# Stepwise mixers, other projection groups and PSUM scratch in a two-layer hybrid trunk

## The chip, the cores and the metric

The kernel runs on one core of one Trainium2 chip. The metric is the time of one execution in device microseconds. Engines are named as in the profile: PE is TensorE, DVE VectorE, ACT ScalarE, POOL GpSimd, SP SyncE, whose queue issues nearly all DMAs. "Lnn" is a line of the kernel.

## The reference

256 tokens of width 2048 go through two layers. Each layer: a modulation from a condition `c` (adaLN: six vectors of 2048 from one product with `ada_w`), RMSNorm, one input projection whose columns feed three mixers side by side, head norm and gates, one output projection, and an MLP with squared ReLU. Everything is fp32.

```python
def hybrid_mixer(h, positions, w_in, conv_w, ..., merge_scale, w_out):
    proj = h @ w_in
    (rq, rk, rv, rg, fq, fk, fv, ff, mq, mk, mv, mo, mi, mf) = jnp.split(proj, IN_SPLIT_IDX, axis=-1)
    y_ret = head_norm(retention(heads(rq), heads(rk), heads(rv), positions)) * jax.nn.silu(rg)     # 4 heads
    y_fox = head_norm(forgetting_attention(heads(fq), heads(fk), heads(fv), ff + fox_f_bias))      # 8 heads
    mqk = jax.nn.silu(causal_conv(jnp.concatenate([mq, mk], axis=-1), conv_w, conv_b))
    mq, mk = jnp.split(mqk, 2, axis=-1)
    y_m = head_norm(mlstm(heads(mq), heads(mk), heads(mv), mi + ..., mf + ...)) * jax.nn.sigmoid(mo)  # 4 heads
    y = jnp.concatenate([y_ret, y_fox, y_m], axis=-1) * merge_scale
    return y @ w_out
```

## The kernel before

**Products.** Activations lie transposed, 16 feature tiles of 128 x 256 tokens. Each fp32 product is made of three passes over rounded halves: an operand is split into a high part and the remainder, and TensorE adds high x low, low x high and high x high. Weights come as 512 KB chunks of two feature tiles by 512 columns (`chunk`): SP issues the DMA into one of six `raw` buffers, ACT rounds to `wh` (L228), and DVE or POOL subtracts to `wl` (L234); `pool_*` in `CFG` is POOL's share. A block is 512 output columns: form B (`mm_b`, L259 to L261) takes 12 matmuls of 256 columns for each feature tile, form A (`mm_a`, L270 to L272, for v, g and o blocks) six of 512.

**Modulation.** One tile of 128 values of `c @ ada_w` is two DMAs of 512 KB into one of four `ada` buffers (the first four halves go to `raw`), and two DVE instructions L292 that multiply by the broadcast condition and sum up. `mod_fix` folds the partial sums on PE (L302, L303) and ends on DVE (L307) or ACT (L305). Tiles wait in a list; `pump` issues them at a rate set by `ada_*` and calls `mod_fix` as soon as a set is issued.

**Order.** `run` first sums the squares of x (L364 to L369, over partitions with ones on PE, L377), forms 1/rms by three Newton steps on DVE (`newton`, L351 to L353), and spreads it with two matmuls (L395). `layer` then goes through w_in in groups of feature tiles, so that it can begin with the first tiles before the whole modulation is there: `h_make` normalises and modulates the group's tiles (L471, L476) and splits them into `hh` and `hl` (L479); `gate_mm` multiplies them with the 76 gate columns; then each of the 14 blocks but the `late` ones takes its partial product, and DVE adds it to the block's sum in SBUF, in two halves of 512 (L521). The late blocks run over all 16 tiles after that. With the last group the mixers start: convolution (L673), gates (L538 to L557), the heads of retention, mLSTM and fox, one PSUM bank `mx` for each head at a time (scores, transposes L635, values L596), `head_norm` with statistics (L708, L709) and normalisation on ACT (L724), `head_out` with transposes on PE (L738) and a merge on DVE (L741). Then come w_out in four blocks with the residual (L750), the first MLP product in two groups, and the rest of the MLP. In layer 1 the input projection is one group and POOL takes no subtractions.

A scheduler orders the instructions of each engine when the kernel is built, from the written order and its own cost estimates; `high_priority` around `mixers` and `gates` moves these ahead, `WIN` holds an ada DMA behind a weight DMA. Each engine then works its row strictly in order.

**Buffers.** PSUM has eight banks of 512 columns: four `pj` (two for each block), two for the condition, two `mx` for everything small.

## Time and profile before

| | |
|---|---|
| time, median of 3 runs | 2559.64 us (2557.45 to 2563.83) |
| profiled execution, time / span | 2560.86 / 2559.1 us |
| PE busy | 2437.6 us (95%), 18996 matmul records |
| DVE busy | 1576.2 us (62%) |
| ACT busy | 1188.3 us (46%) |
| POOL busy | 843.5 us (33%) |
| DMA | 630.46 MB, mean 246 GB/s |
| mean granted clock of PE | 0.98 |

Busy time is a share of the whole span; what an engine costs a stage is read from windows of that stage. Ends of matmuls are modelled: at full flow their records overlap, so PE's time for one is taken from counts in a full window. PEclk is the clock that the throttle granted, 1.00 being 2.4 GHz and half of it the lower level.

### The profile page before, as it was taken

To read this page: it belongs to the slowest core of one execution; us is meant where nothing else is said; L and a number is where in the kernel's file an instruction comes from. 1 tells how busy PE (TensorE), PEld (TensorE's weight loads), DVE (VectorE), ACT (ScalarE), POOL (GpSimd) and SP (SyncE) were. 2 spreads that over 40 slices of the span, in tenths; PEclk is the share of its full clock that TensorE was granted. 3 is DMA by queue.
4 is the path that set the end of the run, shared out by engine and by line. 5 is a ranking of instruction groups with operands and counts; after the bars stand their busy time and mean duration, and the time that the engine had idled before them with its cause. 6 is when DMAs were issued, how large, how long until landed. Compare 5 with 4: busy or idle time off the path is not lost.

```text
span 2559.1 us, 46654 instructions
## 1 busy us (share of the span) xinstructions
PE 2437.6 (95%) x18996; PEld 2365.6 (92%) x18996; DVE 1576.2 (62%) x2468; ACT 1188.3 (46%) x1502; POOL 843.5 (33%) x350
## 2 busy tenths in 40 slices
PE   6999897798999999999999999999999999999997
PEld 5899775798999999999998899989999999999997
DVE  6886985888565453334368976566755554554555
ACT  5444444445553444443455554454654444344443
POOL 4777762234676667666661000000000000000000
PEclk9999997899999999999999999999999999999999
DMA  9899765898999987777776778555555555555553
GB/s 340 301 331 332 232 232 192 316 340 313 346 334 327 333 307 271 262 275 275 261 248 236 253 243 296 173 170 177 187 184 183 187 182 184 187 183 184 186 184 106
DMA packets 177824, 630.46 MB, mean 246 GB/s; under 512 B 19652, under 2 KB 25158, under 8 KB 177608
## 3 DMA queue, kind: packets, MB, share of 16 engines
q1 hardware_dynamic: 177176, 627.08, 70.7%
q8 instruction: 149, 2.44, 0.4%
q14 instruction: 67, 0.55, 0.1%
q10 hardware_dynamic: 432, 0.39, 0.1%
HBM read 625.30 MB, written 2.10 MB: 245 GB/s over the span
## 4 chain that ended last, share of the span: by engine, by line
PE 80%; DVE 11%; issue 2%; POOL 2%; DMA 2%; ACT 2%; SPq 0%; DVEq 0%; POOLq 0%; ACTq 0%
PE pj L260 23%; PE pj L259 23%; PE pj L261 22%; DVE ada L292 3%; PE pj L270 2%; PE pj L271 2%; PE pj L272 2%; POOL wl L234 2%; DMA ada<-ada_w 2%; DVE wl L234 1%; DVE cv L673 1%; PE mx L596 1%; DVE blk L521 0%; DVE blk L417 0%; ACT wh L228 0%
## 5 line engine op out<-in xcount | busy, mean ns | idle before, releaser
L228 ACT CAST wh<-raw 128x1024 fp32r<-128x1024 f32 (+1 forms) x808 | 841.1, 1042 | 1131.1 <-PE pj L261 931.3
L234 POOL TENSOR_TENSOR wl<-raw,wh 128x1024 fp32r<-128x1024 f32 x345 | 840.9, 2444 | 516.7 <-ACT wh L228 506.3
L234 DVE TENSOR_TENSOR wl<-raw,wh 128x1024 fp32r<-128x1024 f32 (+1 forms) x463 | 569.7, 1231 | 550.6 <-ACT wh L228 548.9
L260 PE MATMUL pj<-hh,wl 128*128 128x256 f32 x2912 | 823.0, 285 | 10.3 <-DVE wl L234 7.6
L261 PE MATMUL pj<-hh,wh 128*128 128x256 f32 x2912 | 820.0, 284 | 0.0
L259 PE MATMUL pj<-hl,wh 128*128 128x256 f32 x2912 | 799.5, 285 | 19.9 <-DVE blk L521 9.6
L260 PE MATMUL pj<-blk,wl 128*128 128x256 f32 x2528 | 706.8, 282 | 1.9 <-DVE wl L234 1.9
L261 PE MATMUL pj<-blk,wh 128*128 128x256 f32 x2528 | 704.3, 281 | 0.0
L259 PE MATMUL pj<-blk,wh 128*128 128x256 f32 x2528 | 691.9, 282 | 1.9 <-ACT blk L518 1.5
L260 PEld LDWEIGHTS pj<-hh,wl 128*128 128x128 f32 x2912 | 562.6, 193 | 11.9 <-DVE wl L234 8.2
L259 PEld LDWEIGHTS pj<-hl,wh 128*128 128x128 f32 x2912 | 549.7, 193 | 23.7 <-DVE hl L479 7.8
L261 PEld LDWEIGHTS pj<-hh,wh 128*128 128x128 f32 x2912 | 562.3, 193 | 0.3
L292 DVE SCALAR_TENSOR_TENSOR ada<-ada,cond 128x1024 f32<-128x1024 f32 x380 | 455.7, 1213 | 169.1 <-DMA ada<-ada_w 167.9
L260 PEld LDWEIGHTS pj<-blk,wl 128*128 128x128 f32 x2528 | 477.2, 189 | 2.5 <-DVE wl L234 2.5
L261 PEld LDWEIGHTS pj<-blk,wh 128*128 128x128 f32 x2528 | 477.9, 189 | 0.0
L259 PEld LDWEIGHTS pj<-blk,wh 128*128 128x128 f32 x2528 | 468.3, 189 | 2.5 <-ACT blk L518 1.8
L1005 POOL TENSOR_TENSOR blk<-blk,R 128x1024 f32<-128x1024 f32 x1 | 2.3, 2346 | 1192.0 <-ACT R L399 1192.0
L750 DVE SCALAR_TENSOR_TENSOR X<-pj,mod,X 128x256 f32<-128x256 f32 x284 | 118.2, 476 | 61.3 <-PE pj L261 61.1
L271 PE MATMUL pj<-wl,hh 128*128 128x512 f32 x384 | 154.3, 402 | 0.8 <-POOL wl L234 0.7
L272 PE MATMUL pj<-wh,hh 128*128 128x512 f32 x384 | 152.4, 397 | 0.0
L270 PE MATMUL pj<-wh,hl 128*128 128x512 f32 x384 | 143.8, 401 | 5.3 <-DVE blk L521 3.9
L521 DVE SCALAR_TENSOR_TENSOR blk<-pj,blk 128x512 f32<-128x512 f32 x110 | 74.0, 683 | 38.8 <-PE pj L261 29.0
(216 smaller groups left out, 1672.2 us busy)
## 6 DMA issues: line engine op xcount, KB each, us to landing
raw<-w_ff SPq DMA_DIRECT2D x508, 512.0 KB, 4.1
ada<-ada_w SPq DMA_DIRECT2D x380, 512.0 KB, 6.2
raw<-w_in SPq DMA_DIRECT2D x224, 512.0 KB, 4.9
raw<-w_out SPq DMA_DIRECT2D x64, 512.0 KB, 5.1
X<-x SPq DMA_DIRECT2D x4, 512.0 KB, 6.9
raw<-ada_w SPq DMA_DIRECT2D x4, 512.0 KB, 10.0
raw<-w_ff SPq DMA_DIRECT2D x8, 256.0 KB, 3.6
out<-blk SPq DMA_DIRECT2D x4, 512.0 KB, 3.6
```

Of the source, the lines that this page charges most:

```text
L228: nc.scalar.copy(hi, raw)
L234: eng.tensor_tensor(lo, raw, hi.bitcast(F32), ALU.subtract)
L259: nc.tensor.matmul(o, lhsT=wh[:, s], rhs=al, start=st, stop=False, skip_group_check=True)
L260: nc.tensor.matmul(o, lhsT=wl[:, s], rhs=ah, start=False, stop=False, skip_group_check=True)
L261: nc.tensor.matmul(o, lhsT=wh[:, s], rhs=ah, start=False, stop=last, skip_group_check=True)
L270: nc.tensor.matmul(o, lhsT=al[:, s], rhs=wh, start=first, stop=False)
L271: nc.tensor.matmul(o, lhsT=ah[:, s], rhs=wl, start=False, stop=False)
L272: nc.tensor.matmul(o, lhsT=ah[:, s], rhs=wh, start=False, stop=last)
L292: nc.vector.scalar_tensor_tensor(raw, raw, 1.0, self.cond, ALU.mult, ALU.mult, accum_out=self.part[l][:, i, h:h + 1])
L521: nc.vector.scalar_tensor_tensor(d, p, scale, d, ALU.mult, ALU.add)
L596: nc.tensor.matmul(ps[:, i * P:i * P + P], lhsT=lt, rhs=v[:, j, c:c + P], start=first, stop=last, skip_group_check=True)
L750: V.scalar_tensor_tensor(self.X(k), ps[n // 2][:, n % 2 * T:n % 2 * T + T], self.mod[l][:, c:c + 1], self.X(k), ALU.mult, ALU.add)
```

## The change

- The groups of w_in in layer 0 are 2, 2, 2, 4 and 6 tiles instead of 2, 2, 2, 2, 4, 4, with 12 blocks in each instead of 11: `fv1` is no longer late. Rates of modulation tiles and POOL's shares change (`CFG`).
- The first four modulation tiles (two of scale, two of shift) are computed on PE: `ada_first`, 64 matmuls of one column from weights laid out anew (`ada_0`), eight DMAs of 512 KB that use four `raw` and four `ada` buffers. The ada halves that went to `raw` are gone.
- `pump` leaves `mod_fix` to `flush`, which runs at the next step; the h tiles of the other early tiles are made there.
- A block's two banks are one tile `pj` of 1024 columns, and its sum is one DVE instruction (or one ACT copy) of 1024 columns instead of two of 512.
- `gate_mm` runs once, in the last group. Gates, Newton chains, head norm statistics and the first layer's h tiles have operands in `mx` banks in PSUM instead of SBUF.
- The mixers are generators. `tick` moves up to two of them a step after each chunk of two tiles in `proj`, and in w_out; w_out's products call `tick` until the group that they need is there. The priorities, `DEFER`, `EARLY` and `BEHIND` are gone.

```diff
-CFG = [dict(win=[2, 2, 2, 2, 4, 4], late=3, lead_win=False, ada_win=[4, 4, 4, 8, 8, 16], ada_late=0, ada_out=36,
+CFG = [dict(win=[2, 2, 2, 4, 6], late=2, lead_win=False, ada_win=[4, 4, 8, 12, 14], ada_late=4, ada_out=19,
             ff1=[8, 8], ff1_blocks=6, early_ff1=[[0, 1]], stat_ff1=(0, 1), ada_ff1=[16, 16], ada_ff=48,
-            pool_win=1.0, pool_out=0.5, pool_ff=0.8),
+            ..., ada_ff=60,
+            pool_win=[1.0, 1.0, 1.0, 1.0, 0.5], pool_late=0.5, pool_out=0.3, pool_ff1=[0.3, 0.8], pool_ff=0.8),
...
-NPJ = 4
-DEFER = ("fv1",)
+LANES = 2
-EARLY = 4
-BEHIND = 6
-PRI = dict(mix=1000)
...
     def pump(self, n):
+        self.flush()
...
             if last:
-                self.mod_fix(l, j, kts, {1: C_NMIX, 4: C_NMLP}.get(j))
+                self.fixes.append((l, j, kts))
...
+    def flush(self):
+        while self.fixes:
+            l, j, kts = self.fixes.pop(0)
+            self.mod_fix(l, j, kts, {1: C_NMIX, 4: C_NMLP}.get(j))
+            if (l, j) == (0, 0):
+                self.h_make(0, 0, 1, kts, True)
+
+    def ada_first(self, kts):
+        nc = self.nc
+        ps = self.bank((P, 512))
+        n = len(kts)
+        for i in range(2 * n):
+            for h in range(2):
+                raw = (self.raw if h else self.adap).tile([P, 8, P], F32, tag="raw" if h else "ada", name=self.name("raw"))
+                nc.sync.dma_start(raw, self.io["ada_0"][:, i, 8 * h:8 * h + 8, :])
+                for k in range(8):
+                    nc.tensor.matmul(ps[:, i:i + 1], lhsT=raw[:, k, :], rhs=self.ccol[:, 8 * h + k:8 * h + k + 1],
+                                     start=i == 0 and h == 0 and k == 0, stop=False, skip_group_check=True)
...
+        nc.vector.scalar_tensor_tensor(a[:, KT + kts[0]:KT + kts[0] + n], ps[:, 0:n], 1.0,
+                                       self.vcol(0, C_NMIX + kts[0], n), ALU.add, ALU.mult)
+        nc.scalar.copy(a[:, kts[0]:kts[0] + n], ps[:, n:2 * n])
...
-    def newton(self, v, shape):
+    def newton(self, v, shape, ps, scale=None):
...
+        y = ps[:, :n] if len(shape) == 2 else ps[:, :n].rearrange("p (a b) -> p a b", b=shape[2])
...
     def proj(...):
...
+            w = self.chunk(self.io["w_in"][l, b, k0 // 4][:, r0:r0 + 2, :], 2)
...
+            if late:
+                self.step()
+            self.tick()
...
-            for d, p in zip(self.halves(dst), ps):
-                nc.vector.scalar_tensor_tensor(d, p, scale, d, ALU.mult, ALU.add)
+            d = self.flat(dst)
+            nc.vector.scalar_tensor_tensor(d, ps, scale, d, ALU.mult, ALU.add)
...
     def fox(...):
...
+            yield True
             for b in range(3):
                 nc.tensor.transpose(ps[:, b * P:b * P + P], p[:, b * P:b * P + P], self.ident)
             V.tensor_copy(p, ps[:, 0:384])
+            yield True
             self.pv(ps, p, v, h * P)
             self.u_out(U, h, ps)
+            yield True
...
-        return U, rs
+        self.head_norm(U, rs)
+        yield False
+        yield from self.head_out(l, U, None, 1 + g)
...
     def head_norm(self, U, rs):
-        mv = self.small.tile([P, 2, 4, 2], F32, name="mv")
+        ps = self.bank((P, 512))
+        mv = ps[:, 0:16].rearrange("p (a b c) -> p a b c", b=4, c=2)
...
+    def tick(self):
+        n = 0
+        for t in list(self.tasks):
+            if n == LANES:
+                break
+            r = next(t, None)
+            if r is None:
+                self.tasks.remove(t)
+            else:
+                n += r
...
             if last:
-                with self.tc.high_priority(offset=PRI["mix"]):
-                    self.gates(l, gps)
+                self.gates(l, self.gate_mm(l))
...
                 w = self.chunk(io["w_out"][l, nb, kc], 4)
+                while kc not in self.Y:
+                    self.tick()
...
+                    if j % 2 == 1:
+                        self.tick()
```

The order of the built kernels at three places follows. Tiles are named with numbers; a name keeps its buffer kind (`raw`, `ada`, `mx`, `pj`, `blk`).

DVE before, at the start: the last two of eight ada halves, and what leads to `hl`, which the first w_in matmul reads.

```order
L292 SCALAR_TENSOR_TENSOR ada_195,part_124<-ada_195,cond 128x1024
L292 SCALAR_TENSOR_TENSOR ada_198,part_124<-ada_198,cond 128x1024
L234 TENSOR_TENSOR wl_215<-raw_212,wh_214 128x152
L471 TENSOR_TENSOR ht_206<-X_91,R 128x512
L471 TENSOR_TENSOR ht_650<-X_91,R 128x512
L307 SCALAR_TENSOR_TENSOR mod_126<-mx_190,vec 128x2
L479 TENSOR_TENSOR hl<-ht_206,hh 128x512
```

DVE of the changed kernel at the same place; `mod_129<-mx_173` is the result of the 64 matmuls of `ada_first`. One ada half, ada_351, stands ahead of these rows.

```order
L282 SCALAR_TENSOR_TENSOR ada_354,part_127<-ada_354,cond 128x1024
L282 SCALAR_TENSOR_TENSOR ada_423,part_127<-ada_423,cond 128x1024
L282 SCALAR_TENSOR_TENSOR ada_426,part_127<-ada_426,cond 128x1024
L282 SCALAR_TENSOR_TENSOR ada_483,part_127<-ada_483,cond 128x1024
L282 SCALAR_TENSOR_TENSOR ada_486,part_127<-ada_486,cond 128x1024
L282 SCALAR_TENSOR_TENSOR ada_548,part_127<-ada_548,cond 128x1024
L282 SCALAR_TENSOR_TENSOR ada_551,part_127<-ada_551,cond 128x1024
L344 SCALAR_TENSOR_TENSOR mod_129<-mx_173,vec 128x2
L282 SCALAR_TENSOR_TENSOR ada_779,part_127<-ada_779,cond 128x1024
L282 SCALAR_TENSOR_TENSOR ada_782,part_127<-ada_782,cond 128x1024
L297 SCALAR_TENSOR_TENSOR mod_129<-mx_522,vec 128x2
L505 TENSOR_TENSOR hl<-mx_258,hh 128x512
```

Ten ada halves of later tiles and a second modulation now stand ahead of `hl`.

SP before, behind the DMAs of x: the first 11 transfers of weights.

```order
L291 DMA raw_172<-ada_w 128x1024
L291 DMA raw_175<-ada_w 128x1024
L291 DMA raw_178<-ada_w 128x1024
L291 DMA raw_181<-ada_w 128x1024
L291 DMA ada_184<-ada_w 128x1024
L291 DMA ada_187<-ada_w 128x1024
L291 DMA ada_195<-ada_w 128x1024
L291 DMA ada_198<-ada_w 128x1024
L490 DMA raw_212<-w_gate 128x152
L246 DMA raw_226<-w_in 128x1024
L246 DMA raw_261<-w_in 128x1024
```

SP of the changed kernel, behind x and the eight pieces of `ada_0`, which take all `ada` and four `raw` buffers.

```order
L242 DMA raw_265<-w_in 128x1024
L242 DMA raw_298<-w_in 128x1024
L281 DMA ada_351<-ada_w 128x1024
L242 DMA raw_331<-w_in 128x1024
L242 DMA raw_358<-w_in 128x1024
L281 DMA ada_354<-ada_w 128x1024
L242 DMA raw_391<-w_in 128x1024
L281 DMA ada_423<-ada_w 128x1024
L242 DMA raw_430<-w_in 128x1024
L281 DMA ada_426<-ada_w 128x1024
L242 DMA raw_451<-w_in 128x1024
L281 DMA ada_483<-ada_w 128x1024
```

Each of these ada halves stands behind a w_in chunk, and both take buffers that pieces of `ada_0` held; raw_430 takes that of the last piece.

PE before, where the last head of fox group 1 of this stretch ends and its transposes lead to the next late block.

```order
L596 MATMUL mx_3570<-blk_512,pt_3579 128x128 x3
L635 MATMUL mx_3590<-ident,pt_3599 128x128 x3
L596 MATMUL mx_3590<-blk_512,pt_3599 128x128 x3
L738 MATMUL mx_3669<-ident,blk_512 128x128
L738 MATMUL mx_3674<-ident,blk_512 128x128
L738 MATMUL mx_3669<-ident,blk_512 128x128
L738 MATMUL mx_3674<-ident,blk_512 128x128
L738 MATMUL mx_3679<-ident,blk_512 128x128 x2
L270 MATMUL pj_4323<-wh_4327,hl 128x512
```

PE of the changed kernel after the last late block, `mo`: a fox head's end, the transposes of a fox group and w_out's first product.

```order
L665 MATMUL mx_3930<-ident,pt_3939 128x128 x3
L625 MATMUL mx_3930<-blk_650,pt_3939 128x128 x3
L786 MATMUL mx_3984<-ident,blk_546 128x128
L786 MATMUL mx_4015<-ident,blk_546 128x128
L786 MATMUL mx_3984<-ident,blk_546 128x128 x3
L786 MATMUL mx_4015<-ident,blk_546 128x128 x3
L255 MATMUL pj_4354<-blk_3961,wh_4357 128x256
```

The heads and transposes have moved behind the late blocks, directly ahead of w_out.

## Rows read from the trace of the kernel before

**Rows 1.** The page: span, and the busy share in 40 equal slices, in tenths, with TensorE's granted clock.

```profile
span 2559.1 us, 46654 instructions
...
PE   6999897798999999999999999999999999999997
...
PEclk9999997899999999999999999999999999999999
```

**Rows 2.** Windows: stretch; length, busy us (instructions) by engine, mean TensorE clock, DMA share, GB/s.

```profile
0.00:640.00 640.00, 549.19 (x3750) 506.61 (x3751) 500.79 (x894) 287.13 (x431) 352.90 (x150) 0.94 0.82 293
60.00:90.00 30.00, 23.83 (x167) 22.68 (x166) 28.60 (x40) 13.45 (x21) 16.66 (x8) 0.89 0.76 263
260.00:340.00 80.00, 62.40 (x377) 54.77 (x376) 79.09 (x98) 29.63 (x38) 56.83 (x21) 0.91 0.69 233
340.00:500.00 160.00, 128.29 (x699) 107.73 (x698) 112.47 (x296) 74.00 (x151) 57.36 (x25) 0.85 0.66 237
560.00:600.00 40.00, 33.63 (x275) 32.56 (x274) 34.34 (x58) 15.34 (x24) 16.74 (x7) 1.00 0.80 283
650.00:700.00 50.00, 50.00 (x419) 50.00 (x418) 28.09 (x38) 26.16 (x29) 32.09 (x14) 1.00 0.94 334
1310.00:1480.00 170.00, 155.92 (x1150) 149.28 (x1148) 145.56 (x264) 94.92 (x137) 29.60 (x12) 0.96 0.71 242
```

**Rows 3.** Timeline from the start: start us, duration us, engine, line, operation, [idle before].

```profile
11.09 1.06 ACT L364 ACTIVATE blk<-X 128x1024 f32<-128x1024 f32 x1 [0.20 <-DMA X<-x]
...
14.93 1.86 PE L377 MATMUL mx<-ones,ss 128*128 128x1 f32 x8 [7.11 <-DVE ss L369]
...
21.76 0.16 DVE L353 SCALAR_TENSOR_TENSOR nw<-nw,nw 128x2 f32<-128x2 f32 x1
...
22.35 0.16 DVE L353 SCALAR_TENSOR_TENSOR nw<-nw,nw 128x2 f32<-128x2 f32 x1
...
22.57 1.22 PE L395 MATMUL mx<-ident,nw 128*128 128x128 f32 x4 [5.77 <-DVE nw L353]
...
32.54 0.42 PE L259 MATMUL pj<-hl,wh 128*128 128x256 f32 x1
...
37.19 0.28 PE L260 MATMUL pj<-hh,wl 128*128 128x256 f32 x1
```

**Rows 4.** DMA issues in 0:60: count, KB each, median us from issue to landing.

```profile
ada<-ada_w SPq DMA_DIRECT2D x17, 512.0 KB, 7.8
```

**Rows 5.** Groups of VectorE by line in 0:640: count, busy us, mean ns.

```profile
L292 DVE SCALAR_TENSOR_TENSOR ada<-ada,cond 128x1024 f32<-128x1024 f32 x180 | 216.2, 1211 | 27.1 <-DMA ada<-ada_w 26.7
L521 DVE SCALAR_TENSOR_TENSOR blk<-pj,blk 128x512 f32<-128x512 f32 x110 | 74.0, 683 | 38.8 <-PE pj L261 29.0 <-PE pj L272 9.5
...
L673 DVE SCALAR_TENSOR_TENSOR cv<-blk,vec,cv 128x255 f32<-128x255 f32 (+2 forms) x24 | 20.6, 869 | 0.8 <-ACT cv L671 0.8
...
L544 DVE SCALAR_TENSOR_TENSOR g<-g,g 76x256 f32<-76x256 f32 x7 | 9.8, 1396 | 0.0
...
L741 DVE SCALAR_TENSOR_TENSOR blk<-mx,vec,blk 128x256 fp32r<-128x256 f32 x16 | 7.3, 479 | 10.5 <-ACT blk L740 10.5
```

**Rows 6.** The same groups in 1310:1800, in layer 1.

```profile
L234 DVE TENSOR_TENSOR wl<-raw,wh 128x1024 fp32r<-128x1024 f32 (+1 forms) x140 | 170.1, 1217 | 96.3 <-ACT wh L228 95.8
...
L673 DVE SCALAR_TENSOR_TENSOR cv<-blk,vec,cv 128x255 f32<-128x255 f32 (+2 forms) x24 | 10.8, 475 | 0.1
...
L741 DVE SCALAR_TENSOR_TENSOR blk<-mx,vec,blk 128x256 fp32r<-128x256 f32 x16 | 7.0, 478 | 3.6 <-ACT blk L740 3.6
...
L544 DVE SCALAR_TENSOR_TENSOR g<-g,g 76x256 f32<-76x256 f32 x7 | 2.9, 418 | 0.2
```

**Rows 7.** Timeline of TensorE: two matmuls that waited, with the wait in brackets.

```profile
77.55 0.58 PE L302 MATMUL mx<-part,fold 128*128 128x2 f32 x2 [5.48 <-DVE ada L292]
...
480.98 0.86 PE L738 MATMUL mx<-ident,blk 128*128 128x128 f32 x2 [9.15 <-ACT blk L724]
```

**Rows 8.** Waits of TensorE in 340:490: us in total, times, longest.

```profile
PE mx L738 <- ACT blk L724: 17.5, 4, 9.2
```

More of the change, by code (lines that the diff above doesn't have):

```diff
@@ L431, in lead @@
         nc = self.nc
-        ps = [self.bank(nm="mx" if n < 2 else "pj") for n in range(4)]
+        two, aux = self.pair(), self.pair()
+        ps = [self.bank(), self.bank(), two[:, 0:512], two[:, 512:1024]]
         for c, k0 in enumerate(range(kts[0], kts[-1] + 1, 4)):
             if c == stat_at[0]:
-                self.stat_sum("pj")
+                self.stat_sum(aux)
             if c == stat_at[1]:
-                self.stat_spread("pj")
+                self.stat_spread(aux)
             nk = min(4, kts[-1] + 1 - k0)
@@ L653, in retention @@
             V.tensor_tensor(x, x, sw, ALU.add)
+            yield False
         U = self.heads(v)
@@ L660, in retention @@
             V.tensor_tensor(pt[:, T:384], ps[:, T:384], self.decay[:, h, 0:P], ALU.mult)
+            yield True
             self.pv(ps, pt, v, h * P)
             self.u_out(U, h, ps)
-        return U
+            yield True
+        self.head_norm(U, None)
+        while "rg" not in B:
+            yield False
+        yield False
+        yield from self.head_out(l, U, B.pop("rg"), 0)
     def conv(self, l, x, base):
@@ L823, in layer @@
                     B[nm] = self.proj(l, b, kts, B.get(nm))
-                self.step()
+                if last or b < NA - 3:
+                    self.step()
+                else:
+                    self.flush()
                 if last:
@@ L915, in ff1 @@
             t = acc
-            for d, p in zip(self.halves(t), ps):
-                nc.vector.tensor_tensor(d, p, d, ALU.add)
+            d = self.flat(t)
+            nc.vector.tensor_tensor(d, ps, d, ALU.add)
             nc.scalar.activation(t, t, AF.Relu)
```

262 lines of the change are left out of this document (129 added, 133 removed).

## The prediction

> **What bounds the kernel now.** I read the page first [rows 1]: TensorE is busy in nine tenths or more of nearly every slice; the exceptions are the first slice, three slices around 260 to 500 us and one past the middle. The windows say which stretches have anything to give [rows 2]: in 650:700 TensorE is full at clock 1.00, and 419 matmul records in 50 us make 0.119 us for one of 256 columns; so nothing is to be won there but by fewer matmuls, and the change removes none of the large ones. In 0:640 it is busy for 549.19 of 640 us at a mean clock of 0.94: 91 us idle, plus what the lower of the two levels (1.2 GHz instead of 2.4) costs. A mean of 0.94 is 12% of 640 us, 77 us, at the lower level. The rows at the start show both levels: a 256-column matmul takes 0.42 us at 32.54 and from 37.19 on it takes 0.28 [rows 3]. So the prediction is a sum of the lost time in five stretches of the first 640 us, of one in layer 1, and of what the change puts in place.
>
> **The start (slower by 20).** Before, the last square of x ends at 12.15, the sum over partitions starts at 14.93 and takes 1.86, the Newton chain ends at 22.5 because six ada halves stand between its links, and w_in runs from 32.54 [rows 3]. Now the first four modulation tiles are 64 one-column matmuls on TensorE, and VectorE's order (shown with the change) puts ten ada halves, ada_351 to ada_782 in four buffers, and the modulation of tiles 2 and 3 ahead of `hl`, the operand of the first w_in matmul; before, eight stood there. Their buffers are first held by the weights of the 64 matmuls. Step by step: x's squares added up at about 14.2 (three sums of 0.7 behind 12.15), the sum over partitions 1.9, Newton 13 operations at 0.2 us each (0.59 from one L353 to the next, three operations) 2.6, R 1.2 [rows 3]: the 64 begin at 20. Four one-column matmuls (eight records, two for each in fp32) cost 1.86 at the lower clock [rows 3], so a piece of eight costs 3.7 and all eight pieces 30 us if the level stays low; if it rises after some 6 us of unbroken work, as w_in's did between 32.5 and 37.2, the rest takes half or less, and the end is at 37. The fourth half (ada_426) is queued on SP (its order is shown too) behind a w_in chunk that waits for the last piece's buffer, so it is issued at 37.4 and lands 5 us later in the shallow queue (7.8 is the median in the deep one [rows 4]); the third pair waits for the second pair to be consumed, and ada_782 is worked off at about 51. `hl` and the first w_in matmul follow at 52.5 instead of 32.5: +20. If the low level lasts, the same steps give 64.5 and +32, with the clock +33. Removed there: the gate matmuls of each group but the last (1.2 us each), counted with the boundaries.
>
> **Boundary of the first group (faster by 8).** At 77.55 TensorE stands 5.48 us in the fold of a modulation whose last ada half VectorE has not done [rows 7], and the clock drops: in 60:90, 6.2 us idle and 0.11 x 2 x 30 = 6.6 us at the lower level, half of it lost [rows 2]; 9.5 together. The change issues no ada half in a group's last three blocks and queues the fold a block later (`flush`), so that two to three blocks of 24 matmuls, 2.9 us each, lie between; I leave 1.5. Bounds: -9.5 to 0, since the late halves also pass through this group.
>
> **The last group (faster by 15).** In 260:340 TensorE is idle 17.6 us and VectorE is full with 79.09 of 80; 0.09 x 2 x 80 = 14 us are at the lower clock, of which some 11 busy, 5.5 lost [rows 2]: 23. VectorE is the bound there, partly for being slowed: with POOL's subtractions beside it the conv taps (L673) take 869 ns and the gate chain (L544) 1396 [rows 5], against 475 and 418 in layer 1, where POOL does none [rows 6]; operations with an operand in PSUM don't differ (L741, 479 and 478). What the change does: a group of 6 tiles instead of 4, with 12 blocks, gives TensorE 12 x 72 x 0.119 = 103 us and some 8 of mixers, 111. VectorE has, counted in its order and priced by the undisturbed rows, 30 ada halves (38.7), 19 subtractions (23.2), 12 evictions (14.6; 1.22 each as an L234 of that size, where two took 2 x 0.683), 24 taps (11.4), gates and the rest 20: 108. POOL has half as many subtractions per us, so I add 8 for its disturbance: 116 against 111, a loss of 5, and 3 for uneven order. 23 - 8 = 15. Bounds: 0 to 20.
>
> **Late blocks and mixers (faster by 10).** In 340:500, 31.7 us are idle and 0.15 x 2 x 160 = 48 us at the lower clock, of which some 26 busy, so 13 lost [rows 2]: 45. The largest waits are those of the merge transposes for the normalising activations (L738 for L724, 17.5 us in four [rows 8], 9.15 of it at 480.98 [rows 7]). The stepwise mixers fill the two late blocks well, but the fox heads come last in the queue of tasks. TensorE's order (shown with the change) has the last of them behind the late block `mo`, with w_out next, which needs their transposes; before, a late block stood behind such a piece. From the end of `mo` to the steady flow of w_out VectorE has 57.5 us by its rows: 10 ada halves 12.9, 6 subtractions 7.3, 15 merges (L741) 7.2, and some 30 of statistics, reductions, copies and Newton steps, each by its line's mean. TensorE has 48 w_out matmuls in it (5.7) and 7 of 16 heads; of 35 us for all mixers (128.3 busy, less 66 for three blocks, 13 for the clock and some 14 of w_out) I take 22. So 58 - 28 = 30 are lost, and 5 in the two late blocks: 35 for 45. Bounds: VectorE can run ahead, so that only the heads' own chain is left (-32), or the heads fall in turn on one bank while a head norm holds the other (+8).
>
> **The rest.** w_out: 560:600 has 6.4 us idle [rows 2]; with 19 instead of 36 modulation tiles 3 of it go; 12 of them come back in w_ff, where TensorE is full and VectorE half idle (28.09 of 50 [rows 2]): 0. The lead of ff1: no change within 5. Layer 1, 1310:1480: 14 us idle [rows 2]; the gates without priority and a possible new wait at its last transposes: -1, between -8 and +6. Newton, head norm and gates in PSUM: the rows of L741 show no price of a PSUM operand, so 0. The Trainium skill ("VectorE: DVE Perf Modes", Why PSUM operands drop a tier) speaks against it: an fp32 operation with a PSUM operand gets no faster mode than 1x. No row here shows one operation in both places; by that rule my estimate is at most 1 us for the few one-input steps of the gates and norms, and the sum would be 2545.
>
> **Sum.** 20 - 8 - 15 - 10 - 3 - 1 = -17; from the profiled run's 2560.9 (1.2 over the median): **2544**.
>
> **Rivals.** *Mixers hidden* (0.20): VectorE does its share of the 57.5 us while TensorE is still in `mo`; the heads' chain alone then takes some 36: 22 less, 2522. For it: VectorE is not full in 340:500 (112 of 160 [rows 2]). Against it: the banks, two for all.
> *The start stays at the low clock* (0.16): +33 instead of +20, 2557. For it: the one-column matmuls at 14.93 are the only like work, and short. Against: they run without a gap.
> *The last group stays bound by VectorE* (0.22), the slower side: TensorE needs 111 us, and if the two engines wait for each other as in 260:340, where 62.4 of 80 are busy and 57 useful, the group takes 111/0.78 to 111/0.71, 142 to 156, a loss of 31 to 45 instead of 8; I take 40: 2576. It makes the kernel slower from a group of some 144 us, that is with VectorE at 1.3 times its undisturbed bill; the taps at 869 and the gate chain at 1396 were at 1.8 and 3.3. Against: POOL has fewer subtractions now. The Trainium skill ("GPSIMD Engine Reference", 1. Specifications) says that GpSimd's SBUF interfaces are shared with VectorE, in contention with instructions that have two SBUF inputs; the trace agrees (869 against 475), and by it the conv taps, still in SBUF, stay at 869 while evictions and PSUM chains go free: 24 x 0.39, 9 us on VectorE's 108, 117, about what the sum has.
>
> **How the numbers follow.** Forecast 0.42, its own range 2531 to 2557; rivals 0.20, 0.16, 0.22. A measurement of this kernel can tell 0.3% (7.7 us) from no change: 2553.2 and 2568.5. Faster 0.38 + 0.20 + 0.03 = 0.61; same 0.04 + 0.12 + 0.03 = 0.19; slower 0.01 + 0.19 = 0.20. For 8 in 10 I take 2516 to 2578: a tenth lies below, with the mixers hidden and the boundary better than forecast, and a tenth above, with the last group at its upper price.
>
> **What would show it.** The first w_in matmul at 52 (at 64: the second rival; at 40: my queue was wrong); the gap at the group's boundary gone; the last group 119 long, with TensorE at 0.93 of it (at 0.78 or less: the third rival); some 60 us between `mo`'s last matmul and steady w_out, with VectorE full; the statistic of 650:700 unchanged. It is wrong if TensorE's large matmuls cost other than 0.119, or if w_ff waits for the moved tiles.

## The result, and the profile after

The changed kernel takes 2578.62 us (median of 4 runs, 2576.74 to 2582.11) against 2558.55 for the kernel before in the same runs: a ratio of 1.0076, 95% interval 1.0058 to 1.0095. It is slower by 0.76%, some 20 us, where 2544 was forecast, and lies just outside the range (2516 to 2578).

The page of after: span, TensorE's busy time, and the slices of TensorE and its clock.

```profile
span 2577.0 us, 46671 instructions
...
PE 2468.7 (96%) x19116; PEld 2394.2 (93%) x19116; DVE 1576.0 (61%) x2429; ACT 1183.5 (46%) x1445; POOL 732.8 (28%) x303
...
PE   7999998798999999999999899999999999999997
...
PEclk9999998899999999999999999999999999999999
```

The slices look like those before [rows 1]: no slice shows where 18 us went. TensorE is busier, 2468.7 us instead of 2437.6, and the kernel still ends later: part of that busy time is slow work. The windows of after, in the columns of [rows 2]:

```profile
0.00:640.00 640.00, 573.26 (x3851) 532.31 (x3852) 472.86 (x829) 286.43 (x413) 254.23 (x106) 0.95 0.79 282
...
80.00:100.00 20.00, 14.49 (x86) 13.51 (x85) 17.49 (x26) 8.98 (x14) 9.66 (x4) 0.83 0.74 246
260.00:340.00 80.00, 73.96 (x492) 67.44 (x491) 79.82 (x112) 38.15 (x46) 39.08 (x13) 0.98 0.84 297
340.00:500.00 160.00, 134.55 (x777) 114.62 (x776) 103.02 (x270) 76.31 (x150) 32.06 (x14) 0.87 0.53 184
418.00:492.00 74.00, 48.55 (x246) 38.36 (x245) 43.09 (x139) 34.53 (x84) 2.39 (x1) 0.72 0.26 97
423.70:486.40 62.70, 37.30 (x189) 28.42 (x189) 35.15 (x124) 29.51 (x74) 2.39 (x1) 0.71 0.22 83
560.00:600.00 40.00, 33.77 (x255) 32.91 (x253) 35.34 (x66) 14.51 (x19) 7.22 (x3) 0.91 0.91 324
650.00:700.00 50.00, 50.00 (x419) 50.00 (x419) 31.33 (x40) 25.61 (x26) 27.41 (x13) 1.00 0.95 358
1310.00:1480.00 170.00, 151.98 (x1130) 145.41 (x1129) 136.23 (x241) 89.96 (x127) 31.91 (x14) 0.96 0.70 238
1420.00:1440.00 20.00, 11.81 (x76) 10.80 (x75) 18.81 (x29) 9.32 (x10) 0.00 (x0) 0.82 0.61 204
1720.00:1740.00 20.00, 16.61 (x110) 15.29 (x110) 7.92 (x18) 11.46 (x20) 0.00 (x0) 0.83 0.30 106
```

650:700 is unchanged, to the record (419). 260:340 has 6 us idle instead of 17.6 [rows 2]. The new loss is in places that windows at fixed times compare badly, because the work has moved. So each trace is also cut by work: TensorE's large matmuls, those of 256 and 512 columns with the gates' and mixers' among them, are counted back from the end, at 0.1185 us for 256 columns and 0.228 for 512 (their pitch, from one start to the next, where TensorE is full), and the time between two amounts left is the length of a stage, whatever its start. Smaller matmuls, most of the mixers' work, are not counted, so a stage also gets longer or shorter when they move into it or out of it. The first column is the moment at which 2160 us of them are left, that is behind the start and the first boundary.

| kernel | start | last group (2040 to 1940 left) | late blocks and mixers (1940 to 1860) | w_out, ff1 (1860 to 1740) | layer 1 (1150 to 600) |
|---|---|---|---|---|---|
| before | 116.4 | 136.3 | 151.6 | 153.7 | 656.6 |
| after | 139.4 | 117.2 | 147.7 | 156.1 | 670.4 |
| difference | +23.0 | -19.1 | -3.9 | +2.4 | +13.8 |

The rest adds 1.6 (-0.9 between 2160 and 2040, +1.4 in w_ff of layer 0, +1.1 behind 600), and the sum is the 17.9 us between the two spans. The gain in the last group came; the start and layer 1 cost 36.8 us, nearly twice as much. Each stage time is of one execution: spans of the changed kernel go from 2575.0 to 2580.1, and layer 1 takes 668.2 (e4) to 675.6 (e9) in variants that change nothing in it, so a difference of a few us in one stage is no result by itself.

**The start.** TensorE of after, from the sum over partitions to the first w_in matmul, and VectorE's last steps before it (columns as in [rows 3]):

```profile
13.76 1.86 PE L402 MATMUL mx<-ones,ss 128*128 128x1 f32 x8 [5.46 <-DVE ss L394]
18.23 1.23 PE L420 MATMUL mx<-ident,nw 128*128 128x128 f32 x4 [2.61 <-DVE nw L376]
19.25 27.30 PE L337 MATMUL mx<-ccol,raw 128*128 128x1 f32 x128
...
56.12 0.56 PE L255 MATMUL pj<-hl,wh 128*128 128x256 f32 x1
```

```profile
53.46 1.22 DVE L282 SCALAR_TENSOR_TENSOR ada<-ada,cond 128x1024 f32<-128x1024 f32 x1 [0.73 <-DMA ada<-ada_w]
...
54.68 0.68 DVE L505 TENSOR_TENSOR hl<-mx,hh 128x512 fp32r<-128x512 f32 x1
```

The 64 one-column matmuls (128 records) take 27.30 us without a gap; the tenth ada half is worked off at 54.6, and `hl` and w_in follow, at 56.1 instead of 32.5 [rows 3].

### The profile page after: what moved, and what is told of

Same layout as the page of the kernel before. It is cut to its first block, busy times and chain, and to the rows that moved or that the text cites. A ratio compares the mean times of both kernels' runs of the same rounds, so it can differ in the third digit from the quotient of the medians.

```text
span 2577.0 us, 46671 instructions
## 1 busy us (share of the span) xinstructions
PE 2468.7 (96%) x19116; PEld 2394.2 (93%) x19116; DVE 1576.0 (61%) x2429; ACT 1183.5 (46%) x1445; POOL 732.8 (28%) x303
## 4 chain that ended last, share of the span: by engine, by line
PE 80%; DVE 9%; DMA 3%; issue 3%; POOL 3%; ACT 2%; SPq 0%; DVEq 0%; POOLq 0%; ACTq 0%
PE pj L255 22%; PE pj L256 22%; PE pj L257 22%; PE pj L267 3%; POOL wl L230 3%; PE pj L266 3%; PE pj L268 3%; DVE ada L282 2%; DVE wl L230 2%; DMA ada<-ada_w 2%; PE mx L337 1%; PE mx L625 1%; DMA raw<-w_in 1%; DVE cv L714 1%; ACT wh L224 0%
## 5 line engine op out<-in xcount | busy, mean ns | idle before, releaser
L224 ACT CAST wh<-raw 128x1024 fp32r<-128x1024 f32 x804 | 840.6, 1047 | 1108.6 <-PE pj L257 902.9
L230 DVE TENSOR_TENSOR wl<-raw,wh 128x1024 fp32r<-128x1024 f32 x506 | 622.7, 1232 | 488.4 <-ACT wh L224 487.8
L230 POOL TENSOR_TENSOR wl<-raw,wh 128x1024 fp32r<-128x1024 f32 (+1 forms) x298 | 730.2, 2453 | 635.8 <-ACT wh L224 559.2
L255 PE MATMUL pj<-hl,wh 128*128 128x256 f32 x2912 | 830.4, 285 | 2.2 <-DVE hl L505 1.4
L255 PE MATMUL pj<-blk,wh 128*128 128x256 f32 x2528 | 716.1, 284 | 5.4 <-ACT blk L543 3.0
L256 PE MATMUL pj<-blk,wl 128*128 128x256 f32 x2528 | 715.3, 283 | 5.0 <-DVE wl L230 4.0
L257 PE MATMUL pj<-blk,wh 128*128 128x256 f32 x2528 | 712.7, 282 | 0.0
L255 PEld LDWEIGHTS pj<-hl,wh 128*128 128x128 f32 x2912 | 560.9, 193 | 4.0 <-DVE hl L505 1.9
L255 PEld LDWEIGHTS pj<-blk,wh 128*128 128x128 f32 x2528 | 480.6, 190 | 6.5 <-ACT blk L543 3.5
L257 PEld LDWEIGHTS pj<-blk,wh 128*128 128x128 f32 x2528 | 480.9, 190 | 0.0
L267 PEld LDWEIGHTS pj<-wl,hh 128*128 128x128 f32 x384 | 72.3, 188 | 19.4 <-DVE wl L230 5.2
```

The source lines that it names most:

```text
L224: nc.scalar.copy(hi, raw)
L230: eng.tensor_tensor(lo, raw, hi.bitcast(F32), ALU.subtract)
L255: nc.tensor.matmul(o, lhsT=wh[:, s], rhs=al, start=st, stop=False, skip_group_check=True)
L256: nc.tensor.matmul(o, lhsT=wl[:, s], rhs=ah, start=False, stop=False, skip_group_check=True)
L257: nc.tensor.matmul(o, lhsT=wh[:, s], rhs=ah, start=False, stop=last, skip_group_check=True)
L267: nc.tensor.matmul(o, lhsT=ah[:, s], rhs=wl, start=False, stop=False)
```

## The experiments

All are edits of the changed kernel, and ratios are to the kernel before in the same runs; the changed kernel's own is 1.0076. Stages are those of the table above.

**e1, the start as before.** The edit left out at its head puts the first four ada halves into `raw` buffers again.

```diff
...
-        for k in range(2, KT, 2):
+        for k in range(0, KT, 2):
             self.ada_plan([(0, (1, 0), [k, k + 1])])
...
-        self.ada_first([0, 1])
-        self.h_make(0, 0, 1, [0, 1], True)
```

> The changed kernel with the start of the kernel before: the first four modulation tiles on VectorE again, their first four halves in raw buffers, no one-column matmuls; all else as changed. Theory A (the start is a chain that everything stands behind: 64 matmuls for 27 us at the lower clock hold the buffers of ten ada halves, which stand ahead of the first w_in matmul): that matmul comes at 32 to 34 instead of 55.6, and the whole gains 20 to 23, about 2557. Rival B (the lag is lent: w_in's first groups wait for transfers and modulations anyway, so an earlier start meets them later): the matmul is as early, but the lead over the changed kernel has shrunk under 10 by 250 us, and the time is 2568 or more.

Ratio 1.0008 (0.9997 to 1.0018), 0.68% less than the changed kernel: some 17 us, short of Theory A's 20 to 23. The first w_in matmul comes at 29.5, without the group's gate matmuls even earlier than before:

```profile
29.47 0.58 PE L257 MATMUL pj<-hl,wh 128*128 128x256 f32 x1 [3.55 <-DVE hl L512]
```

24.8 us are won at the first mark and 23.5 are left 100 us later. Theory A holds up to there. In the last group (122.0 instead of 117.2) and the late stretch (150.9 instead of 147.7) 8 are given back: a third of the gain was lent, and two thirds stay.

**e4, the clock in the start.**

```diff
+        dm = self.pair()
+        for i in range(8):
+            nc.tensor.matmul(dm[:, 0:P], lhsT=self.ones, rhs=self.ones, ...)
...
                 for k in range(8):
+                    nc.tensor.matmul(dm[:, 0:P], lhsT=self.ones, rhs=self.ones, ...)
                     nc.tensor.matmul(ps[:, i:i + 1], lhsT=raw[:, k, :], ...)
```

> The changed kernel with added work on TensorE: eight 128-column matmuls of ones ahead of the 64 one-column matmuls, and one ahead of each of them, into a bank that nobody reads. It measures the cost of the clock there. Theory A (the 64 stand at the lower level, 0.427 each, because one-column matmuls do not raise it): the clock rises within the first ten, the added work pays for itself, the 64 with their 64 added ones end no later than 46.4, and the time is within 6 of the changed kernel. Rival B (they are bound by something else than the clock, loading of weights or transfers): the clock rises or not, each pair costs 0.427 plus the added matmul's 0.2 to 0.4, the end moves from 46 to 60 or later, and the time by 10 or more.

Ratio 1.0058 (1.0043 to 1.0073). The scheduler put all the added matmuls ahead of the 64, not among them, which makes the test sharper. TensorE's timeline, and windows with the granted clock (the last but two column):

```profile
8.89 7.41 PE L340 MATMUL pj<-ones 128*128 128x128 f32 x64
...
16.95 5.16 PE L340 MATMUL pj<-ones 128*128 128x128 f32 x44
...
22.39 24.79 PE L341 MATMUL mx<-ccol,raw 128*128 128x1 f32 x128
```

```profile
23.09 2.04 PE L341 MATMUL mx<-ccol,raw 128*128 128x1 f32 x17
...
29.76 3.55 PE L341 MATMUL mx<-ccol,raw 128*128 128x1 f32 x16
```

```profile
22.40:25.00 2.60, 2.60 (x27) 2.60 (x25) 0.70 (x1) 1.42 (x2) 0.12 (x1) 1.00 0.24 95
26.00:47.00 21.00, 21.00 (x100) 21.00 (x100) 7.37 (x12) 1.09 (x2) 5.89 (x3) 0.50 0.89 319
```

Behind the 128-column matmuls the one-column ones start at the upper level, 0.112 us from one to the next (some 16 in the 2 us shown); at 25 the clock falls to 0.50 while TensorE is busy without a gap, and they go at 0.213, as in the changed kernel throughout (27.30 for 128). So Theory A's cause is right, the one-column matmuls stood at the lower level and did not hold the upper one, and its consequence is not: the end moved from 46.4 to 47.2, since the extra work comes first. The start as a whole hardly moves (56.1 to 56.2): the chain of buffers and ada halves behind the 64 sets it.

**e6, the late constants behind the third group.**

```diff
-CONST_AT = 0
+CONST_AT = 2
```

> The changed kernel with the late constants (rotary angles, sine and cosine, masks) made behind the third group of w_in instead of the first. Theory A (the hole at the first group's boundary, 5.5 idle and 6.9 us at the lower clock around 91 to 98, is VectorE's queue: the chain of rotary angles, at 1.3 to 2.7 us each beside POOL, stands ahead of the last two ada halves, which have landed): the hole is gone, 8 to 9 won by 110 us, and kept unless the chain makes one at the third boundary. Rival B (the hole comes from the fold's place or from the late arrival of the halves): the fold at the first boundary waits 3 to 5 us as before.

Ratio 1.0106 (1.0092 to 1.0120). In after the fold at the first boundary waits on two ada halves, and VectorE's timeline shows why they are late:

```profile
90.54 0.38 PE L292 MATMUL mx<-part,fold 128*128 128x2 f32 x2 [3.18 <-DVE ada L282]
...
93.25 0.58 PE L292 MATMUL mx<-part,fold 128*128 128x2 f32 x2 [2.33 <-DVE ada L282]
```

```profile
83.85 2.67 DVE L200 TENSOR_TENSOR rt<-rt 128x256 f32<-128x256 f32 x1
86.44 2.90 DVE L204 SCALAR_TENSOR_TENSOR rt<-rt 128x256 f32<-128x256 f32 x2
89.27 1.21 DVE L282 SCALAR_TENSOR_TENSOR ada<-ada,cond 128x1024 f32<-128x1024 f32 x1
...
90.41 1.65 DVE L204 SCALAR_TENSOR_TENSOR rt<-rt 128x256 f32<-128x256 f32 x1
91.98 1.21 DVE L282 SCALAR_TENSOR_TENSOR ada<-ada,cond 128x1024 f32<-128x1024 f32 x1
```

The halves have no wait in brackets: the rotary angles (`rt`) stand ahead of them on VectorE. It was so in the kernel before, ahead of the half that its fold at 77.55 waited for [rows 7]:

```profile
71.67 2.33 DVE L199 TENSOR_SCALAR rt<-rt 128x256 f32<-128x256 f32 x1
74.04 2.31 DVE L200 TENSOR_SCALAR rt<-rt 128x256 f32<-128x256 f32 x1
76.28 1.21 DVE L292 SCALAR_TENSOR_TENSOR ada<-ada,cond 128x1024 f32<-128x1024 f32 x1
```

With the constants elsewhere TensorE is full there, and the hole has moved to where they are now:

```profile
80.00:100.00 20.00, 20.00 (x147) 19.01 (x146) 7.73 (x12) 13.25 (x16) 16.04 (x8) 1.00 0.83 295
170.00:200.00 30.00, 24.46 (x143) 22.81 (x142) 29.50 (x39) 9.55 (x14) 16.19 (x8) 0.83 0.70 246
```

7.0 won at the first mark, 11.6 lost by 210 us. Theory A on the cause; the place chosen was worse.

**e2, layer 1's mixers and gates at once.** At each call of `mixers` in layer 1 the tasks run until they wait for a block, at raised priority; the gates too.

```diff
+        if l == 1:
+            with self.tc.high_priority(offset=1000):
+                for t in list(self.tasks): ...
...
+                    with self.tc.high_priority(offset=1000):
+                        self.gates(l, ps)
```

> The changed kernel with layer 1's mixers and gates as before: each mixer's steps are issued at once when its last block is there, at raised priority, and the gates too; layer 0 stays stepwise. Theory A (the 13 to 14 us that the changed kernel loses in layer 1 between 1310 and 1900 come from mixers that are spread and end right ahead of w_out, and from gates without priority): the hole at 1720 to 1737 (3.4 idle and 6.9 at the lower clock) is gone, the one at 1420 to 1443 is as before, 10 to 13 gained, 2566. Rival B (the loss is of another part of the change, PSUM scratch or one eviction for two): gain under 4, and the small waits for wl between 1480 and 1560 stay.

Ratio 1.0024 (1.0013 to 1.0035), 0.52% less. Layer 1 takes 662.4 instead of 670.4, and TensorE has no hole ahead of w_out (1720:1740); the one at the gates is nearly as it was:

```profile
1420.00:1440.00 20.00, 11.08 (x73) 10.14 (x72) 18.07 (x28) 9.32 (x10) 0.00 (x0) 0.84 0.56 192
1720.00:1740.00 20.00, 20.00 (x173) 20.00 (x172) 11.95 (x15) 12.78 (x19) 0.00 (x0) 1.00 0.51 181
```

Theory A: the spread mixers cost some 8 of layer 1's 13.8 us. The other 5.8 remain; their largest piece is the wait for `wl` behind the gate chain on VectorE (7.7 us at 1420 to 1443, 5.2 before), and what makes it longer was not parted further.

**e3, the groups of before, and e13, POOL's share alone.**

```diff
-CFG = [dict(win=[2, 2, 2, 4, 6], late=2, ..., ada_win=[4, 4, 8, 12, 14], ada_late=4, ...,
-            pool_win=[1.0, 1.0, 1.0, 1.0, 0.5], ...
+CFG = [dict(win=[2, 2, 2, 2, 4, 4], late=3, ..., ada_win=[4, 4, 4, 8, 8, 16], ada_late=4, ...,
+            pool_win=[1.0, 1.0, 1.0, 1.0, 1.0, 1.0], ...
```

> The changed kernel with the groups of before (2, 2, 2, 2, 4, 4 tiles, 11 blocks, three late ones, their rates of modulation tiles and all subtractions of the groups on POOL); all else as changed. Theory A (the 19 us won between 260 and 350 come from the long last group with half of POOL's share): this loses 15 to 19 of them, 2594 to 2597. Rival B (they come from the single evictions and the PSUM chains, which don't slow under POOL): the last group still keeps TensorE over 0.9 busy and the loss is under 6, 2584 or less.

Ratio 1.0143 (1.0128 to 1.0158); the last group's stage takes 129.5 instead of 117.2. Theory A, with 12 of its 15 to 19, all of it idle time (9.5) and large matmuls above their pitch (2.8). For e13 only the last 0.5 of `pool_win` becomes 1.0.

> The changed kernel with all subtractions of the last group of w_in on POOL, as in the groups before it, instead of every second. It parts the length of the group from POOL's share. Theory A (the share decides, because POOL's work slows VectorE's and POOL itself, 36 subtractions at 2.44 us are 88 of some 110 us, falls behind at times): holes return between 290 and 350, 8 to 16 slower, 2587 to 2595. Rival B (the longer group decides, since the same evictions, taps and gates are spread over half as much TensorE work again): within 4 of the changed kernel.

Ratio 0.9990 (0.9980 to 1.0000): against both, 0.86% less than the changed kernel. The last group's stage takes 131.9 instead of 117.2, and the late stretch 117.0 instead of 147.7. Part of these two differences is work that moved. The two stages hold 270 small matmuls in either kernel; 57 of them stand in the last group's stage of the changed kernel, 143 in that of e13, with three of the eight fox heads. If each matmul is taken to last until the next one starts, the 14.7 us that e13's last group is longer are 8.1 of small matmuls, 3.4 of idle time and 3.2 of large matmuls above their pitch; so Theory A's loss is there, but less than half of it as holes and slower work. Both stages together take 248.9 instead of 264.9: 16.0 are won, not 31. Of these 7.9 are the same 270 small matmuls, which take 29.8 instead of 37.7, and 6.5 are idle time.

POOL's share does nothing by itself in the late stretch (e3 has the full share too, and takes 148.1 there); but with other estimates the scheduler builds another order. In the changed kernel seven of the eight fox heads stand behind the last late block, in e13 two, the others between its matmuls, those of the late block ahead and the last ones of the group. The windows of e13:

```profile
260.00:340.00 80.00, 70.56 (x475) 64.11 (x474) 79.59 (x130) 40.46 (x53) 60.27 (x22) 0.98 0.76 260
340.00:480.00 140.00, 124.53 (x758) 107.38 (x757) 92.55 (x233) 72.13 (x140) 43.16 (x18) 0.94 0.63 223
```

In the changed kernel and all its variants the late stretch goes by that number (the kernel before, with three late blocks and priorities, has two behind and takes 151.6, which this does not explain). The last column has the last group and the late stretch together, so that work moved from one to the other counts for nothing:

| fox heads behind the last late block | late stretch, us | both stages, us |
|---|---|---|
| 8 (e9) | 153.7 | 270.3 |
| 7 (after, e1, e2, e4, e6, e10) | 147.7, 150.9, 147.1, 147.4, 147.8, 150.9 | 264.9, 272.9, 265.8, 265.0, 270.1, 270.2 |
| 6 (e3, e5, e7) | 148.1, 144.0, 140.0 | 277.6, 263.7, 258.0 |
| 4 (e8) | 132.9 | 265.4 |
| 3 (e12) | 132.7 | 266.1 |
| 2 (e13, e15) | 117.0, 119.6 | 248.9, 250.2 |
| 1 (e16, e18) | 116.6, 113.2 | 250.7, 269.0 |

By the late stretch alone a head more behind costs some 6 us; by both stages five heads cost 16.0 (after against e13) or 20.0 us (e10 against e15), 3 to 4 each, with what POOL's larger share costs in the last group taken off. e8, e12 and e18, with the gates' scratch in SBUF, lose in the last group what they win behind it. A head that stands alone lets TensorE wait in turn for VectorE and ACT. These are the waits of TensorE in 418:492 in after (total, times, longest), where VectorE is busy for 43.09 of 74 us in the window above, so not the bound:

```profile
PE mx L786 <- ACT blk L771: 11.8, 6, 9.8
PE mx L625 <- DVE pt L666: 5.6, 5, 3.3
PE mx L665 <- ACT pt L662: 4.3, 4, 1.7
```

The longest of these waits is not a head's own round: the transposes of the last fox group wait for its head norm, whose small steps, with two ada halves ahead of them, keep VectorE busy for 8.80 of the 10.2 us in 472.7:482.9:

```profile
482.86 0.48 PE L786 MATMUL mx<-ident,blk 128*128 128x128 f32 x1 [9.78 <-ACT blk L771]
```

```profile
472.73 1.22 DVE L282 SCALAR_TENSOR_TENSOR ada<-ada,cond 128x1024 f32<-128x1024 f32 x1 [1.75 <-DMA ada<-ada_w]
...
482.11 0.17 DVE L768 SCALAR_TENSOR_TENSOR nb<-mx,nw 128x8 f32<-128x8 f32 x1
```

**e8, the gates' scratch in SBUF.**

```diff
-        sc = self.bank((NG, 512))
+        sc = self.tmp.tile([NG, 512], F32, tag="gsc", name=self.name("g"), bufs=1)
```

> The changed kernel with the gates' scratch in SBUF instead of a PSUM bank; head norm and Newton stay in PSUM. Theory A (beside POOL an instruction with two SBUF inputs takes up to three times as long, and PSUM operands avoid that): in layer 0 the gate chain's polynomial steps rise from 411 ns towards 700 to 1400, the last group loses 2 to 6 us; in layer 1, without POOL, the one-input steps fall from 0.42 to 0.29. Rival B (with half as many subtractions on POOL in the last group nothing is left to avoid): the steps take 0.42 in layer 0 too, and the time is within 3 of the changed kernel.

Ratio 1.0063 (1.0049 to 1.0076), no difference in sum, from two large ones: the last group takes 132.6 instead of 117.2, the late stretch 132.9 instead of 147.7 (four heads behind). Of the first difference 4.4 are small matmuls that moved there; 7.6 are idle time and 3.6 large matmuls above their pitch. The seven polynomial steps in layer 0, first after, then e8:

```profile
L572 DVE SCALAR_TENSOR_TENSOR g<-g,mx 76x256 f32<-76x256 f32 x7 | 2.9, 411 | 0.0
```

```profile
L572 DVE SCALAR_TENSOR_TENSOR g<-g,g 76x256 f32<-76x256 f32 x7 | 9.5, 1361 | 0.0
```

Theory A on the steps: with two SBUF inputs they take 1361 ns beside POOL, with one in PSUM 411, in a group where POOL had half its share.

**e5, two evictions for one.**

```diff
-            nc.vector.scalar_tensor_tensor(d, ps, scale, d, ALU.mult, ALU.add)
+            for h in (0, 512):
+                nc.vector.scalar_tensor_tensor(d[:, h:h + 512], ps[:, h:h + 512], scale, d[:, h:h + 512], ...)
```

> The changed kernel with each block's addition in w_in again in two instructions of 512 columns instead of one of 1024. Theory A (the fixed part of an instruction, 0.15 us a block, counts only where VectorE is full, in the last group: 12 blocks): 0 to 4 slower, 2579 to 2582. Rival B (one eviction for two is what keeps TensorE full in the last group, since it frees both banks at once): TensorE under 0.88 busy in the last group, 8 or more slower.

Ratio 1.0071 (1.0055 to 1.0086): Theory A, the single eviction is worth nothing that can be measured (last group 119.7 instead of 117.2).

**e7, head norm's scratch in SBUF.**

```diff
-        ps = self.bank((P, 512))
+        ps = self.small.tile([P, 64], F32, name="hn")
         mv = ps[:, 0:16].rearrange("p (a b c) -> p a b c", b=4, c=2)
```

> The changed kernel with head norm's scratch (statistics, variance, Newton) in SBUF, so that it holds no mx bank. Theory A (between 418 and 492 the heads go through the one bank that is left while a head norm holds the other): heads come closer together there, 8 or more of the some 40 us lost are won, 2570 or less. Rival B (VectorE's queue and the order of tasks set that stretch, not the banks): within 4 of the changed kernel.

Ratio 1.0041 (1.0026 to 1.0056); the late stretch takes 140.0 instead of 147.7. Theory A, with some 8 us for the held bank, though one head less behind is part of them (e5, with six heads too, takes 144.0).

**e9, layer 0's mixers at once.** The edit of e2 with `l == 0` and without the gates.

> The changed kernel with layer 0's mixers issued at once at raised priority, as in the kernel before, and layer 1 stepwise. Theory A (the stepwise mixers fill TensorE's late blocks in layer 0, where VectorE and POOL are loaded, and are worth what the forecast gave them): the holes come before the late blocks, 360 to 480 loses 10 or more, 2588 and over. Rival B (the order of heads, not their spreading, sets that stretch, and it ends with the same chain ahead of w_out): within 5 of the changed kernel, some holes moved.

Ratio 1.0113 (1.0099 to 1.0127), 0.37% more: the late stretch 153.7 with all eight heads behind, and 5 more in layer 1, which the edit doesn't touch. Theory A: stepwise mixers are worth something in layer 0, but some 6 us, not the whole stretch.

**Together: e10 (e1 and e2) and e12 (and e7, e8).**

> The two undone parts together: start as before, and layer 1's mixers and gates issued at once at raised priority; groups, evictions, PSUM scratch and layer 0's stepwise mixers as changed. Theory A (start and layer 1 are separate costs): the gains of the two single runs add, 0.68% and 0.52% below the changed kernel's 1.0076, so a ratio of 0.9955, some 11 us faster than before. Rival B (the second covers part of the first, since both only let later work wait elsewhere): ratio 0.998 to 1.001.

Ratio 0.9988 (0.9979 to 0.9997), Rival B: layer 1 takes 667.6 here instead of the 662.4 of e2, and the end of the kernel 2.9 more. The gains don't add in full.

> The kernel with the old start and layer 1's mixers and gates at once, and in addition the scratch of head norm and gates in SBUF; groups, evictions and layer 0's stepwise mixers as changed. Theory A (the bank that head norm held is a cost of its own, 0.35% in the single run; the gates' one-input steps are 0.13 us cheaper each in SBUF): ratio 0.994 to 0.996, 10 to 15 us faster than before. Rival B (in this order of work another wait takes its place, as already for the two together, 0.9988 instead of 0.9955): 0.998 to 1.0.

Ratio 0.9959 (0.9946 to 0.9971), Theory A: 11 us faster than before.

**With the late stretch: e15 (e10 and e13), e16 (and e7), e18 (and e8).**

> Old start, layer 1's mixers and gates at once, and all subtractions of the last group on POOL; the rest as changed. TensorE's order has two fox heads behind the last late block here, instead of seven in the changed kernel. Theory A (what the late stretch costs goes by the number of heads that stand alone behind the late blocks: 148 to 151 us with seven, 133 with three or four, 117 with two, from the same amount of work left to the same amount): the stretch takes 115 to 122, and the gains of the single runs add, ratio 0.986 to 0.989. Rival B (in e13 it was POOL's share that emptied VectorE in that stretch, whatever the heads' order, or another wait takes its place with the earlier start): the stretch takes 130 or more, ratio 0.992 or more.

Ratio 0.9896 (0.9882 to 0.9909): 2535.92 us against 2562.88, 27 us faster than the kernel before and 1.8% faster than the changed one. The late stretch takes 119.6, as Theory A had it, the last group 130.5, layer 1 664.8; the ratio is just above its 0.986 to 0.989, so most of the sum of the single gains is there. The windows that hold its last group and its late stretch:

```profile
240.00:320.00 80.00, 70.05 (x470) 63.73 (x469) 78.64 (x122) 40.12 (x52) 59.84 (x22) 0.98 0.77 266
320.00:460.00 140.00, 122.75 (x754) 107.28 (x752) 93.29 (x248) 70.83 (x139) 42.98 (x18) 0.93 0.64 229
```

> As the run before, with head norm's scratch in SBUF; one fox head behind the last late block. Theory A (heads alone and the held bank are two costs): the late stretch takes 110 to 117, ratio 0.984 to 0.988. Rival B (with the heads spread the bank is no cost any more): as the run before, within 0.001.

Ratio 0.9903 (0.9888 to 0.9918), Rival B: the late stretch is 3 shorter and the last group 4 longer; with the heads spread the bank costs nothing that can be measured.

> As the run before, with the gates' scratch in SBUF too; one fox head behind the last late block. Theory A (the gates gain in PSUM only beside a busy POOL, which they have here again, since all subtractions of the last group are on POOL): the polynomial steps take over 0.8 us in layer 0, some 10 us of VectorE more in the last group, ratio 0.003 worse than the run before. Rival B (they are hidden by the blocks of the group): the same within 0.001.

Ratio 0.9971 (0.9959 to 0.9982): worse by 0.007, more than Theory A's 0.003. The last group takes 155.8 instead of 134.1, and 15.4 of these 21.7 are idle time of TensorE. With POOL at its full share the gates' SBUF chain holds VectorE up where it is the bound; the seven steps, and the longest wait of TensorE in that stage, which is for the gates' result `H`:

```profile
L579 DVE SCALAR_TENSOR_TENSOR g<-g,g 76x256 f32<-76x256 f32 x7 | 7.2, 1035 | 0.0
```

```profile
PE mx L604 <- DVE H L591: 8.0, 1, 8.0
```

## Why the prediction was wrong

*The start*, forecast +20, measured +23.6 (56.1 against 32.5): right as a chain, with its first matmul between the two cases of 52.5 and 64.5, but that the number came near is in part luck. The forecast let the clock rise and the 64 matmuls end at 37; the clock stayed low, as in the second rival, and they ended at 46.5 (27.3 us, where 30 was worked out). From there to the first matmul it took 9.6 us where the forecast had 15.5, since six of the ten ada halves were done beside them; so the second rival's price was too high.

*The first boundary*, forecast -8, measured nothing: the lag is 23.0 behind it. The failed step is "TensorE stands in the fold of a modulation whose last ada half VectorE has not done": true as a row [rows 7], but the cause lay further back. The half was late because the rotary angles stood ahead of it on VectorE, before as after. The change moved the fold and not the angles, and the hole stayed; e6 moved the angles, and it left that place.

*The last group*, forecast -15, measured -19.1: right, with VectorE full (79.82 of 80 us) and TensorE at 0.92 of 260:340, and by its reasons, apart from the evictions: groups and POOL's share together are worth 12 (e3), the gates in PSUM some 11 (e8, without the small matmuls that moved), POOL's share by itself 6.6 (e13, likewise); these are not a sum. The third rival, that VectorE would hold TensorE at 0.78 or less, did not happen; that its 2576 lies nearest to the measured time is chance.

*Late blocks and mixers*, forecast -10, measured -3.9. The failed step is the price, VectorE's "57.5 us by its rows", taken as what the stretch lasts. From the end of `mo` (423.7) to the steady flow of w_out (486.4) it lasts 62.7, near the "some 60" that was expected, but not by VectorE's work: VectorE is busy for 35.15 of them. What the waits show is a round between three engines for each fox head that has no large matmuls beside it, and the last head norm, 9.8 us by itself. The order named the seven heads, and the number was there to be priced by the heads, as the bound +8 had begun to do. That no kernel moves the heads and nothing else leaves one doubt: the price of a head rests on variants in which other edits moved them.

*w_out and ff1*, forecast -3, measured +2.4: 560:600 has 6.2 us idle, as before (6.4 [rows 2]), so the 3 us were not won; why was not looked for. *Layer 1*, forecast -1 between -8 and +6, measured +13.8: the term that turned the sign, with the boundary. The failed step is "the gates without priority and a possible new wait at its last transposes": the wait came, and was priced too low. Around it, between 800 and 780 us of work left (1716 to 1746 us in after), the changed kernel takes 8.1 longer, of which 3.4 are idle time, 2.5 large matmuls above their pitch and 2.2 small ones; the gates' hole grew by 2.5, and small waits came between. e2 wins 8.0 of the 13.8 back, but the same edit only 4.9 in e10 (667.6 against 672.5 in e1); the rest stays open.

In sum the forecast missed by 8 at the boundary, 15 in layer 1, 6 in the late stretch, 5 in w_out and 3 in the start, and won 4 in the group: 33 of the 35 us between 2544 and 2578.6. Undoing the start and layer 1 together takes the loss away (e10, 0.9988).

## What to carry to other kernels

A wait names the last releaser, not the reason: before a fold or a priority is moved, read the row of the engine that released it, back to what stood ahead there. Work that no large matmuls stand beside is priced by its round of waits, not by its busiest engine; count from the built order how many such rounds stand alone. Where a scheduler orders by estimates, an edit in one stage can reorder another (0.5 to 1.0 in POOL's share took 31 us off a stretch that has little of POOL in it, and put 15 on the stage ahead, more than half of them moved work), so each edit is measured alone, and by stage, before it is judged; and where stages are cut by counted work, see whether the work that is not counted has moved from one to the next.

## What the runs showed of the hardware

One-column fp32 matmuls did not hold TensorE's upper clock: in e4 they began at 0.112 us a record at 1.00 and went on at 0.213 at 0.50, without a gap between; in the changed kernel they ran at 0.213 for 27 us. The granted clock is written as 1.00 ahead of the first change in a trace (1.00 for 0:20 and 20:40 of after, where the records say the lower level), so there the durations have to be read.

VectorE beside POOL's subtractions: 1361 ns for a step with two SBUF inputs (e8), 411 with one of them in PSUM (after; 409 in e16, where POOL has all subtractions), and 418 for two SBUF inputs without POOL [rows 6]. The Trainium skill ("GPSIMD Engine Reference", 1. Specifications) names this contention for instructions with two SBUF inputs, and the runs agree. The price of PSUM shows in layer 1, where POOL is idle, on the gates' first one-input step, of e8 (SBUF) and after (PSUM):

```profile
L566 DVE TENSOR_SCALAR g<-g 76x256 f32<-76x256 f32 x1 | 0.3, 289 | 0.1
```

```profile
L566 DVE TENSOR_SCALAR mx<-g 76x256 f32<-76x256 f32 x1 | 0.4, 424 | 0.1
```

That is the rule that the prediction held against the PSUM scratch ("VectorE: DVE Perf Modes", Why PSUM operands drop a tier, in the Trainium skill), and the rows agree with it. It costs 0.135 us a step, about 1 us for the gates of one layer, where at most 1 us was estimated for all. Against it stand the some 17 us (0.9971 against 0.9903, e18 and e16) that the same scratch saves where POOL has all subtractions.
